# Low halves of some weights made by an accumulating DMA instead of a GpSimd subtraction, in a two-layer hybrid DeltaNet/Hyena/FNet trunk

## The chip, the cores and the metric

One core of one Trainium2 chip. The metric is the device time of one execution in microseconds (us), and what counts is the median over runs.

## The reference, cut to what matters

Two layers with shared weights run over 128 context tokens and 512 latent tokens (640 columns in all, fp32). The first half of each layer multiplies the normalised input `h` by the wide matrix `w_in` and feeds the pieces of the product to three mixers:

```python
proj = h @ p['w_in']                       # columns: qkv | z | b | a | hyena | fnet | 3 gates
y_a, s_fin = delta_mixer(proj[qkv], proj[z], proj[b], proj[a], ...)   # gated DeltaNet, both directions
y_b = hyena_mixer(proj[hyena], ...)
y_c = fourier_mixer(proj[fnet])
merged = gates[0] * (y_a @ w_pa) + gates[1] * (y_b @ w_pb) + gates[2] * (y_c @ w_pc)
x = x + g1 * (merged @ w_o)                # then x = x + g2 * swiglu(norm(x))
```

The DeltaNet is a scan over chunks of 64 tokens, forwards and backwards, and each chunk needs a triangular inverse first.

## The kernel before

**Weights.** A weight matrix comes as blocks of 128 output columns: one transfer of 512 KB on SP's queue into a raw tile `wr` (two buffers). TensorE takes each fp32 operand as a high and a low part in a reduced format (`F32R`), with three matmuls for each product: high by high, high by low, low by high (`mm3`). So each 512-column half of a raw block, called a unit, is split by `wsplit`: ScalarE copies it with rounding into `hi` (tile `wh`), and GpSimd subtracts, `lo = src - hi` (tile `wl`). There are four buffers of each, two blocks' worth. After the last matmuls of a block, `free` emits the splits of the block after the next. A unit is then waiting for TensorE to let go of its buffers, for its raw data, for ScalarE and for GpSimd, in that order.

**The two stretches in question.** After the qkv blocks, `mixer` starts the DeltaNet as four coroutines (`delta`: three of preparation, one scan). While they run, the main program multiplies blocks that don't depend on them: four for the Fourier mixer, four for `z`, twelve for the Hyena input, and eight for the first gate. These 28 blocks of each layer have 56 units, 112 in both layers. The scan's preparation is mostly VectorE work: `delta_inv` inverts the triangular blocks with 110 small elementwise instructions on tiles `A` for each batch, plus 32x32 transposes. GpSimd makes masks and scaled copies for it. VectorE also does the short convolutions of the Hyena blocks (`T<-T,par,T`), whose results SP stores (`hyS`) before it issues the next weight load that stands behind in its queue.

**Order.** The whole program is emitted by a planner at build time: each emitted instruction advances a clock of its engine by a modelled cost (`tick`), and a coroutine's next step is emitted between main-line matmuls when its data should be there by these clocks (`pump`). On the chip each engine works through its own list in that order.

The lines at the centre, from `wsplit`:

```python
nc.scalar.copy(hi[:, :w], src)
nc.gpsimd.tensor_tensor(out=lo[:, :w], in0=src, in1=hi[:, :w].bitcast(F32), op=ALU.subtract)
self.whl[self.nunit] = (hi, lo)
```

The planner's price of a transfer is its bytes at 360 GB/s behind the other transfers, with 2 us to land; that of a GpSimd `tensor_tensor` of 512 columns is 1.24 us.

Of the kernel before, what the change touches and what calls it, by code (L numbers as in the profile page):

```python
# [9 lines left out]
F32 = mybir.dt.float32  # L10
F32R = mybir.dt.float32r
I32 = mybir.dt.int32
AF = mybir.ActivationFunctionType
ALU = mybir.AluOpType
# [5 lines left out]
D = 1024  # L20
# [19 lines left out]
OFF_BA = 2048  # L40
OFF_HY = 2080
OFF_FN = 3616
OFF_G = 4128
# [6 lines left out]
def _stream():  # L50
    s = [("ba", 0)] + [("in", m * P) for m in QKV_ORDER]
    s += [("in", OFF_FN + m * P) for m in range(4)]
    s += [("in", 1536 + m * P) for m in range(4)]
    s += [("in", OFF_HY + m * P) for m in range(12)]
    gate = lambda br, m: ("in", OFF_G + BR[br] * D + m * P)
    s += [gate("a", m) for m in range(8)]
    s += [gate("c", 0), gate("c", 1)]
    s += [("pa", m) for m in range(0, 8, 2)]
    s.append(("pc", 0))
    for m in range(2, 8, 2):  # L60
        s += [gate("c", m), gate("c", m + 1), ("pc", m)]
    s += [gate("b", m) for m in range(8)]
    s += [("pb", m) for m in range(0, 8, 2)]
    s += [("o", m) for m in range(8)]
    for j in range(NFF):
        s += [("g", j), ("u", j)]
    for g in range(len(GROUPS)):
        s += [("d", g, m) for m in range(0, 8, 2)]
    return s


def _plan():

    p = [("w", k) for k in _stream() if k[0] not in ("g", "u", "d")]
    for kind, g in _ffn_order():
        if kind == "gu":
            for j in GROUPS[g]:
                p += [("s", j)] if j >= WHOLE else [("w", ("g", j)), ("w", ("u", j))]
        else:
            p += [("w", ("d", g, m)) for m in range(0, 8, 2)]  # L80
    return p
# [9 lines left out]
def _parked(key):  # L91

    k, m = (key[0], key[-1]) if isinstance(key, tuple) else (None, None)
    return (k == "o" and m >= O_SPLIT or k in ("g", "u") and m == 1 or k == "in" and m // P in QKV_ORDER[1:Q_SPLIT]
            or k == "d" and key[1] == len(GROUPS) - 1 and m >= D_SPLIT)


def _width(key):
    if key[0] == "ba":
        return 256  # L100
    if key[0] == "d":
        return 2 * len(GROUPS[key[1]]) * P
    return 1024
# [195 lines left out]
class _Net:  # L299
# [191 lines left out]
    def wplan(self, depth):  # L491

        keys = {k: n for n, k in enumerate(_stream())}
        self.raws, self.units, self.items = [], [], []
        self.parked = set()
        for l in range(depth):
            for kind, k in _plan():
                r, u = len(self.raws), len(self.units)
                if kind == "w":
                    w = _width(k)  # L500
                    c = 512 if k[0] != "d" else w // 2
                    self.raws.append((l, keys[k], w))
                    self.units += [(r, "raw", i, min(c, w - i)) for i in range(0, w, c)]
                else:
                    self.raws += [(l, keys["g", k], 1024), (l, keys["u", k], 1024)]
                    self.units += [(r, x, 0, 512) for x in SEVEN]
                self.items.append((k, u, len(self.units)))
                if _parked(k):
                    self.parked.update(range(u, len(self.units)))
        self.rlast = {r: n for n, (r, x, *_) in enumerate(self.units) if x[0] != "s"}  # L510
        self.wt = {}
        self.spent, self.sums, self.whl = {}, {}, {}
        self.qs = False
        self.nraw = self.nunit = self.item = self.nseen = self.nout = 0
        self.lot = []
# [26 lines left out]

    def wsplit(self, n):

        nc = self.nc
        while self.nunit <= n:
            r, x, c0, w = self.units[self.nunit]
            self.wload(r if x == "raw" else r + 1)
            if x == "raw":
                src = self.wt[r][:, c0:c0 + w]  # L550
            elif x[0] == "a":
                src = {"a11": self.wt[r][:, :512], "a12": self.wt[r][:, 512:], "a22": self.wt[r + 1][:, 512:]}[x]
            else:
                src = self.wsum(r, x)
            if self.nunit in self.parked:
                hi, lo = self.lot.pop(0)
            else:
                assert self.nout < 4
                self.nout += 1
                hi = self.pw.tile([P, 512], F32R, tag="wh", name=self.nm("wh"), bufs=4)  # L560
                lo = self.pw.tile([P, 512], F32R, tag="wl", name=self.nm("wl"), bufs=4)
            nc.scalar.copy(hi[:, :w], src)
            nc.gpsimd.tensor_tensor(out=lo[:, :w], in0=src, in1=hi[:, :w].bitcast(F32), op=ALU.subtract)
            self.whl[self.nunit] = (hi, lo)
            if x[0] == "a":
                for y in {"a11": ("s2", ), "a22": ("s3", "s4"), "a12": ()}[x]:
                    self.wsum(r, y)
            if self.rlast[r] == self.nunit:
                self.spent[r] = self.spent[r if x == "raw" else r + 1] = self.when(lo)
            if x == "s4":  # L570
                self.sums = {}
            self.nunit += 1
# [1653 lines left out]
```

## Time and profile before

| | |
|---|---|
| median of 3 runs | 2834.18 us (2827.09 to 2837.05) |
| the profiled execution | 2837.89 us, its span 2836.1 us |
| mean granted TensorE clock | 0.949 |
| busy: PE, PEld, DVE, ACT, POOL | 2566.9, 2434.9, 1856.7, 1017.8, 1332.8 us |
| the two stretches (first Fourier block to the output of the DeltaNet) | about 243 to 610 us and 1655 to 2000 us |

PE is TensorE's matmuls, PEld its weight loads, DVE is VectorE, ACT ScalarE, POOL GpSimd, SP the queue that issues most transfers. An arrow `a<-b,c` gives the output and input tiles of an instruction. A wait `X <- Y` is time in which X stood idle and that ended with an instruction of Y. Busy time of a matmul is modelled, and grows when the clock that the chip grants TensorE falls.

### The profile page before, as it was taken

The page shows a single profiled execution, that of the slowest core. Times are in us where ns is not written, and L with a number is a line of the kernel's source. Part 1 is how long each engine was busy: PE and PEld are TensorE (multiplying, and loading weights), DVE is VectorE, ACT ScalarE, POOL GpSimd, SP SyncE. Part 2 cuts the span into 40 slices and gives each one's busy share as a digit, 9 for nine tenths or more (in the row PEclk, how much of TensorE's full clock was granted, in tenths as well). Part 3 has the DMA queues.
Part 4 walks back from the last instruction along what each step waited for, and adds up shares of the span by engine and source line. Part 5 has one row for each costly group of instructions (what it writes and reads, how often), then busy time and mean ns, then how long its engine had stood idle before and what let it go on. Part 6 is the DMA issues. An engine that isn't in the chain of part 4 may idle for free. (4 is left out here: it accounts for less than half of the span.)

```text
span 2836.1 us, 55639 instructions
## 1 busy us (share of the span) xinstructions
PE 2566.9 (91%) x22520; PEld 2434.9 (86%) x22520; DVE 1856.7 (65%) x3417; ACT 1017.8 (36%) x2175; POOL 1332.8 (47%) x1228
## 2 busy tenths in 40 slices
PE   5898779788999999999988979698899989999998
PEld 3687779788998888999977778687889989999997
DVE  5466987544654484767665789784555347877765
ACT  4454224232332342433435532332323323444432
POOL 2234426242335464666742444353423345767662
PEclk8999989899999999999999989798999999999999
DMA  7541221333564246222222312213336442222222
GB/s 288 178 143 56 69 77 56 115 120 122 180 234 148 84 129 216 91 81 89 84 84 97 121 54 79 78 58 98 115 138 243 152 156 65 71 83 83 82 75 82
DMA packets 109552, 324.18 MB, mean 114 GB/s; under 512 B 10202, under 2 KB 24538, under 8 KB 102816
## 3 DMA queue, kind: packets, MB, share of 16 engines
q1 hardware_dynamic: 107856, 312.76, 32.8%
q0 software_dynamic: 1440, 7.87, 0.8%
q8 instruction: 177, 2.90, 0.4%
q14 instruction: 79, 0.65, 0.1%
HBM read 288.60 MB, written 37.24 MB: 115 GB/s over the span
## 5 line engine op out<-in xcount | busy, mean ns | idle before, releaser
L2175 PE MATMUL pg<-A,wh 128*128 128x320 f32 (+1 forms) x6304 | 1473.2, 321 | 52.2 <-DVE T L2175 15.3
L2175 PEld LDWEIGHTS pg<-A,wh 128*128 128x128 f32 (+1 forms) x6304 | 1082.0, 194 | 98.1 <-POOL A L2175 18.6
L2175 POOL TENSOR_TENSOR wl<-wr,wh 128x512 fp32r<-128x512 f32 (+2 forms) x486 | 680.0, 1413 | 769.6 <-ACT wh L2175 730.7
L2175 PE MATMUL pg<-A,wl 128*128 128x320 f32 (+1 forms) x3152 | 997.7, 317 | 0.3 <-POOL wl L2175 0.2
L2175 PEld LDWEIGHTS pg<-A,wl 128*128 128x128 f32 (+1 forms) x3152 | 610.2, 194 | 3.6 <-POOL wl L2175 2.7
L2175 ACT CAST wh<-wr 128x512 fp32r<-128x512 f32 (+2 forms) x486 | 286.3, 612 | 442.9 <-PE pg L2175 341.4
L2175 PE MATMUL ps<-A,wh 128*128 128x320 f32 x1696 | 378.0, 309 | 0.0
L2175 PEld LDWEIGHTS ps<-A,wh 128*128 128x128 f32 x1696 | 283.4, 188 | 1.4 <-issue 1.2
L2175 PE MATMUL ps<-A,wl 128*128 128x320 f32 x848 | 262.9, 310 | 4.6 <-POOL wl L2175 4.4
L2175 PE MATMUL ps<-A,A 32*32 32x32 f32 (+5 forms) x2984 | 215.1, 251 | 52.9 <-DVE A L2175 51.0
L2175 POOL TENSOR_TENSOR wl<-U,wh 128x512 fp32r<-128x512 f32 x160 | 226.6, 1432 | 48.0 <-ACT wh L2175 48.0
L2175 PEld LDWEIGHTS ps<-A,A 32*32 32x32 f32 (+2 forms) x2984 | 186.4, 154 | 66.3 <-DVE A L2175 52.2
L2175 DVE TENSOR_TENSOR A<-A 128x120 f32<-128x120 f32 (+22 forms) x690 | 216.1, 375 | 11.0 <-DMA A<-hyS 8.0
L2175 DVE TENSOR_TENSOR T<-T,T 128x320 f32<-128x320 f32 (+1 forms) x139 | 130.3, 937 | 86.0 <-ACT T L2175 81.8
L2175 POOL TENSOR_TENSOR A<-A,A 128x640 fp32r<-128x640 f32 (+5 forms) x84 | 121.0, 1453 | 112.5 <-ACT A L2175 111.6
L2175 PEld LDWEIGHTS ps<-A,wl 128*128 128x128 f32 x848 | 159.2, 188 | 7.0 <-POOL wl L2175 7.0
L2175 PE MATMUL pg<-A,A 128*128 128x320 f32 x1056 | 160.9, 310 | 0.0
L2175 ACT CAST wh<-U 128x512 fp32r<-128x512 f32 x160 | 99.1, 620 | 162.8 <-PE ps L2175 64.2
L2175 PEld LDWEIGHTS pg<-A,A 128*128 128x128 f32 x1056 | 156.1, 188 | 0.7 <-issue 0.2
L2175 DVE STREAM_TRANSPOSE A<-A 32x1024 f32<-32x1024 f32 x72 | 148.9, 2093 | 1.3
L2175 DVE TENSOR_TENSOR U<-ps,U 128x512 f32<-128x512 f32 x144 | 78.0, 543 | 104.2 <-PE ps L2175 66.3
L2175 DVE SCALAR_TENSOR_TENSOR A<-pg,mod,A 128x320 f32<-128x320 f32 (+2 forms) x152 | 72.8, 492 | 84.9 <-PE pg L2175 84.6
(163 smaller groups left out, 3021.1 us busy)
## 6 DMA issues: line engine op xcount, KB each, us to landing
wr<-in_wbig_dram SPq DMA_DIRECT2D x272, 512.0 KB, 3.6
A<-in_wmod_dram SPq DMA_DIRECT2D x40, 1024.0 KB, 5.3
A<-hT SPq DMA_DIRECT2D x32, 1024.0 KB, 7.1
kSp<-U SPq DMA_DIRECT2D x40, 256.0 KB, 2.1
U<-kSp SPq DMA_DIRECT2D x40, 256.0 KB, 6.0
A<-in_wmod_dram SPq DMA_DIRECT2D x16, 512.0 KB, 10.2
hyS<-T SPq DMA_DIRECT2D x24, 320.5 KB, 3.1
wr<-in_wbig_dram SPq DMA_DIRECT2D x16, 384.0 KB, 3.2
```

The source lines that it names most:

```text
L2175: return f(*a, **k)
```

## The change

For units whose block is in the `z`, Hyena, Fourier or first-gate part of `w_in`, ScalarE first writes `-src`, rounded, into `lo`. Then a transfer issued by GpSimd adds `src` to `lo` in place, from `wr` in on-chip memory to `wl` in on-chip memory, 256 KB each. Only then ScalarE makes `hi`. All other units keep the subtraction.

```diff
+def _added(key):
+
+    return isinstance(key, tuple) and key[0] == "in" and (1536 <= key[1] < OFF_BA or OFF_HY <= key[1] < OFF_G + D)
...
-        self.parked = set()
+        self.parked, self.added = set(), set()
...
+                if _added(k):
+                    self.added.update(range(u, len(self.units)))
...
-            nc.scalar.copy(hi[:, :w], src)
-            nc.gpsimd.tensor_tensor(out=lo[:, :w], in0=src, in1=hi[:, :w].bitcast(F32), op=ALU.subtract)
+            if self.nunit in self.added:
+                nc.scalar.activation(lo[:, :w], src, AF.Copy, scale=-1.0)
+                nc.gpsimd.dma_start(lo[:, :w], src, accum_op=ALU.add)
+                nc.scalar.copy(hi[:, :w], src)
+            else:
+                nc.scalar.copy(hi[:, :w], src)
+                nc.gpsimd.tensor_tensor(out=lo[:, :w], in0=src, in1=hi[:, :w].bitcast(F32), op=ALU.subtract)
```

## Rows read from the trace of the kernel before

**Rows 1.** Busy time by engine, from the page: time, share of the span, instructions.

```profile
PE 2566.9 (91%) x22520; PEld 2434.9 (86%) x22520; DVE 1856.7 (65%) x3417; ACT 1017.8 (36%) x2175; POOL 1332.8 (47%) x1228
```

**Rows 2.** Windows: length, busy PE, PEld, DVE, ACT, POOL; granted clock, DMA share, GB/s.

```profile
243.00:400.00 157.00, 128.07 (x1291) 121.94 (x1293) 135.45 (x302) 47.50 (x108) 73.20 (x89) 0.89 0.23 74
400.00:610.00 210.00, 185.35 (x3192) 172.03 (x3183) 128.55 (x237) 66.83 (x161) 88.85 (x100) 0.91 0.26 83
1655.00:1815.00 160.00, 127.79 (x1349) 121.58 (x1350) 142.99 (x319) 44.10 (x105) 70.09 (x88) 0.86 0.22 71
1815.00:2000.00 185.00, 166.43 (x2934) 155.33 (x2934) 117.19 (x227) 61.41 (x146) 87.55 (x92) 0.92 0.24 74
```

**Rows 3.** Waits of PE, 243 to 400 us: total us, times, longest.

```profile
PE ps L2175 <- DVE A L2175: 13.2, 1, 13.2
PE pg L2175 <- DVE T L2175: 9.3, 6, 3.5
PE ps L2175 <- POOL U L2175: 5.8, 2, 5.6
```

**Rows 4.** Waits of PE, 1655 to 1815 us.

```profile
PE ps L2175 <- DVE A L2175: 14.5, 1, 14.5
PE ps L2175 <- DVE U L2175: 7.6, 2, 7.4
PE pg L2175 <- DVE T L2175: 6.0, 4, 2.8
PE ps L2175 <- POOL U L2175: 5.7, 2, 5.5
```

**Rows 5.** Waits of PE for VectorE, 400 to 610 us, then 1815 to 2000 us.

```profile
PE ps L2175 <- DVE A L2175: 14.1, 7, 4.8
...
PE ps L2175 <- DVE A L2175: 14.6, 6, 5.5
```

**Rows 6.** Groups of VectorE, the inverse's elementwise work: 243 to 400, 1655 to 1815 us.

```profile
L2175 DVE TENSOR_TENSOR A<-A 128x126 f32<-128x126 f32 (+25 forms) x217 | 62.6, 351 | 1.0
...
L2175 DVE TENSOR_TENSOR A<-A 128x126 f32<-128x126 f32 (+25 forms) x217 | 63.6, 356 | 0.9
```

**Rows 7.** The same work by shape, 243 to 400 us, two shapes.

```profile
L2175 DVE TENSOR_TENSOR A<-A 128x128 f32<-128x128 f32 x8 | 1.8, 284 | 0.0
...
L2175 DVE TENSOR_TENSOR A<-A 128x15 f32<-128x15 f32 x2 | 0.3, 171 | 0.0
```

**Rows 8.** Groups of GpSimd, the subtractions, 243 to 400 us.

```profile
L2175 POOL TENSOR_TENSOR wl<-wr,wh 128x512 fp32r<-128x512 f32 x28 | 36.3, 1315 | 51.1 <-ACT wh L2175 42.5 <-PE pg L2175 8.6
```

**Rows 9.** Timeline, 285 us: start, duration, engine, instruction, count.

```profile
284.79 2.48 POOL L2175 TENSOR_TENSOR wl<-wr,wh 128x512 fp32r<-128x512 f32 x2
285.10 4.25 DVE L2175 TENSOR_TENSOR A<-A 128x31 f32<-128x31 f32 x4
```

**Rows 10.** DMA issues: queue, count, KB each, median us from issue to landing.

```profile
A<-in_wmod_dram SPq DMA_DIRECT2D x16, 512.0 KB, 10.2
...
U<-in_cd_dram POOLq DMA_DIRECT2D x2, 256.0 KB, 4.4
U<-in_nptab_dram POOLq DMA_DIRECT2D x2, 256.0 KB, 5.2
```

**Rows 11.** GpSimd's time for issuing such a transfer: ns min/median/max.

```profile
L2175 POOL DMA_DIRECT2D U<-in_cd_dram x2: 607/608/609, 628.2 to 2021.1; - x2
```

**Rows 12.** ScalarE's rounding copies: ns min/median/max.

```profile
L2175 ACT CAST wh<-wr x486: 389/619/757, 36.6 to 2777.3; 128x512 fp32r<-128x512 f32 x150, 128x384 fp32r<-128x384 f32 x10, 128x256 fp32r<-128x256 f32 x2
```

**Rows 13.** Timeline, 355 to 395 us, GpSimd and TensorE's weight loads.

```profile
363.22 2.55 POOL L2175 TENSOR_TENSOR wl<-wr,wh 128x512 fp32r<-128x512 f32 x2 [8.57 <-PE pg L2175]
...
366.65 0.19 PEld L2175 LDWEIGHTS pg<-A,wl 128*128 128x128 f32 x1
...
367.09 0.19 PEld L2175 LDWEIGHTS pg<-A,wl 128*128 128x128 f32 x1
...
384.40 1.60 PEld L2175 LDWEIGHTS ps<-A,A 32*32 32x32 f32 x62 [13.28 <-DVE A L2175]
```

## The prediction

> **What bounds the kernel now.** Start with the page's busy times. TensorE (PE) is busy 91% of the span [rows 1], so over the whole kernel there are some 270 us to win, and only where PE stands still. The windows then show the two stretches in which the 112 affected units are split and used [rows 2]. In the first part of each (243 to 400 us and 1655 to 1815 us) VectorE is busy 135 of 157 and 143 of 160 us, and PE 128 in both, at a granted clock of 0.89 and 0.86. In the second parts PE is busy 88 to 90% of the time and VectorE about 62%. So in the first parts the work that sets the pace is VectorE's, in the second parts mostly PE's. PE's waits say the same [rows 3, 4]: in the first part of layer 0 it waits 13.2 + 9.3 us for VectorE and 5.8 us for GpSimd; in layer 1, 14.5 + 7.6 + 6.0 and 5.7 us. The big single waits of 13 to 15 us end when `delta_inv` has done its second batch. Row [rows 13] shows that place in layer 0: weight loads stop for 13.28 us until 384.40. In the second parts 14.1 and 14.6 us of such waits are left, in pieces of at most 5.5 us [rows 5].
>
> Next, what a subtraction on GpSimd does to VectorE. By shape, an elementwise instruction of the inverse takes 171 ns for 15 elements and 284 ns for 128 [rows 7]: about 156 ns and 1 ns an element. A batch has 110 of them with 10,912 elements (from the loop in `delta_inv`), so a mean of 255 ns when nothing is in the way. The windows show 351 and 356 ns over 217 of them [rows 6]. The excess is (351 - 255) x 217 = 21 us in layer 0 and 22 us in layer 1. What is in the way can be read from the timeline [rows 9]: while GpSimd makes two weight subtractions (2.48 us), four VectorE instructions of 31 elements take 4.25 us, where 4 x 0.187 = 0.75 us were to be expected. So VectorE stands still inside its instructions while GpSimd reads two tiles of on-chip memory.
>
> **The change part by part.**
> *Removed: 112 subtractions.* 28 of them lie in the first part of layer 0, at 1.3 us each, 36.3 of GpSimd's 73 us there [rows 8, 2]; layer 1 does the same work. How much of the 21 and 22 us of excess is theirs? At least their share of GpSimd's busy time, a half: 10.5 and 11 us. At most all of it. They come without regard to what VectorE does, while the scan's own GpSimd work mostly stands before or after the VectorE work of its batch, so I take a value nearer the upper end, 17 us for each layer. The waits for VectorE that it can shorten are 22.5 and 28.1 us in the same windows [rows 3, 4], so it fits into them: 34 us in both layers, with bounds of 21 and 43.
> *Freed: GpSimd's queue.* An issue takes 0.6 us [rows 11] where a subtraction took 1.3, so masks and scaled copies behind it start some 0.7 us sooner for each unit, and PE's two waits for GpSimd (5.8 and 5.7 us, behind two subtractions each) shrink by 1.4 us each. In the second parts the same relief meets a PE that is busy: of 28.7 us of waits for VectorE [rows 5] I count a tenth. Together 3 + 3, say 5 us, with bounds of 0 and 29.
> *Added: 112 rounding copies on ScalarE*, 0.62 us each [rows 12], 69 us. ScalarE is busy 220 of the 712 us [rows 2], so they lie in its idle time. What is queued behind a pair is the eviction of the block's last result and the scan's copies, later by up to 1.2 us. I count nothing; without that cover all 69 us would come on top.
> *Added: 112 transfers.* The trace has none from on-chip memory to on-chip memory and none that adds. The nearest are GpSimd's casting loads of the same 256 KB: 4.4 and 5.2 us from issue to landing [rows 10]. A 512 KB load, which moves the bytes that an add must read, took 10.2 us where it had company [rows 10]. I take 5.2, nearer to the first, since the source is on the chip; 4.4 and 10.2 are the bounds. The low part then is there 0.6 + 5.2 us after ScalarE's write, where the subtraction took 1.3: 4.5 us later. Who waits? PE, if the low part was ready by less than that. In the tightest place of layer 0 that I found, a subtraction pair starts at 363.22, its first unit is done at 364.50, and PE first loads it at 366.65 [rows 13]: 2.15 us of slack, so PE would stand for 2.4 us. But 18 us later PE waits 13 us for VectorE in any case. I allow for two or three like places in each layer. I count 5 us for both layers, between 1 and 8; where the first parts' waits vanish, these stalls are what appears. The raw buffer `wr` is let go 4.5 us later too; its next load stands in SP's queue behind the Hyena stores, which wait for VectorE longer than that, so nothing is added.
> *Not moved on purpose, but moved:* the planner reckons with another price and another engine, so the order of scan steps between the main blocks will differ a little. I have no row for that; it is some us either way.
> *Against:* a rule speaks for a smaller transfer cost than the row. The Trainium skill, DMA: Bandwidth & Descriptors, section Anatomy of one DMA, gives a fit of about 2.0 us and the bytes at 436 GB/s; as an estimate that is 2.6 us for 256 KB. By it no place would run short and the sum would be 5 us lower. The row has 4.4 us for the same size, so the row decides.
>
> **Sum.** -34 - 5 + 5 = -34 us. From the profiled execution, 2837.9 us (span 2836.1 and 1.8 around it), that is 2804. The median of the runs shown is 3.7 us lower, which would give 2800. I forecast 2802 us.
>
> **The rivals.**
> *A, slower: the transfers land too late.* At PE's own pace a block takes 16 weight loads of low parts, 0.44 us apart [rows 13], 7.0 us. A unit's buffers come free up to 1.8 us before the block ends that used them, and it is needed a block later: 8.8 us, of which copy and issue take 1.2. So a landing of L costs nothing up to 7.6 us when blocks follow each other; above that a block loses between half of the rest and all of it (the lead is two blocks), three quarters on the mean. 28 x 7.0 = 197 us of a stretch of 367 are such blocks, so I count half of the 56: 21 x (L - 7.6). With L = 10.2 [rows 10] that is 55 us against 39 gained: 2854. It turns slower than before from L = 9.5. For it: an add reads twice. Against: 4.4 us for a cast of the same size. Chance 0.15.
> The Trainium skill, Collectives: The Full Stack, section The bandwidth ceiling, says that a reducing transfer runs at half the rate of a copy because it needs two source reads. Taken as a doubling of the whole 4.4 us, A would cost 21 x 1.2 = 25 us and the time would be 2824; no trace here shows an add.
> *B, no change: VectorE's time isn't on the path.* The 217 instructions get shorter, but PE fills the time with its own blocks, whose loads pass through SP's queue behind VectorE's convolutions. For it: PE is busy 128 of 157 us; against: the waits of 22 and 28 us. Gain 5, cost 5: 2838. Chance 0.12.
> *C, much faster:* all 43 us of excess go, the second parts' 29 us of waits too, cost 5: 2771. For it the granted clock, 0.85 to 0.93 in these windows, would rise as the waits shrink; against it the second parts' full PE. Chance 0.10.
> *D, the change does only half:* GpSimd's writing of the transfer's descriptors holds VectorE up as its subtraction did, for 0.6 of 1.3 us. Then 18 + 3 - 5 = 16 us: 2822. Chance 0.13.
>
> **How the numbers follow.** My own case has 0.50 and spans 2785 (43 + 5 of gain, 1 of cost, and 6 for the clock) to 2822 (21 of gain, 5 of cost). A change of 0.3%, 8.5 us, is what a measurement here can tell from none. Faster: 0.50 + 0.10 + most of D, 0.71. Same: most of B and some of D, 0.12. Slower: A and the rest of B, 0.17. The range goes down to 2772, which takes in nearly all of C, and up to 2840, which takes in B and leaves out most of A: about 0.18 outside.
>
> **What would show it.** Right: in the first parts the inverse's 217 instructions take about 275 ns instead of 351, the single waits of 13 to 15 us are gone or under 3 us, the second parts hardly change, the transfers land in 4.4 to 6 us, and few new waits of PE name a transfer into `wl`. Wrong: a landing above 7.6 us and PE's weight loads waiting for it (A); waits for VectorE as before, with shorter VectorE work (B); VectorE's instructions still long beside GpSimd's issues (D); or losses outside the two stretches, which only a changed order could explain.

## The result and the profile after

The changed kernel took 2784.23 us (median of 4 runs, 2778.55 to 2790.82) beside 2830.64 us (4 runs) for the kernel before: a ratio of 0.9843, 95% interval [0.9821, 0.9865], so 1.6% or 46 us faster. The forecast was 2802 us and faster, with 2772 to 2840 as its range.

First the page of the changed kernel: the busy times that answer to [rows 1], GpSimd's group of issues, and the transfer's line among the DMA issues (count, KB, median us from issue to landing).

```profile
PE 2552.8 (92%) x22520; PEld 2422.3 (87%) x22520; DVE 1805.7 (65%) x3417; ACT 1076.0 (39%) x2287; POOL 1267.5 (46%) x1228
...
L2188 POOL DMA_DIRECT2D wl<-wr x112 | 98.0, 899 | 272.3 <-ACT wl L2188 258.8
...
wl<-wr POOLq DMA_DIRECT2D x112, 256.0 KB, 4.7
```

VectorE has exactly as many instructions as before, 3417, and needs 51 us less for them: it did the same work with less standing still. TensorE's busy time fell by 14 us at a granted clock of 0.957 (before 0.949). The transfers land in 4.7 us at the median (forecast 5.2); an issue holds GpSimd for 0.90 us (forecast 0.6).

Next the groups of VectorE in the changed kernel, over two spans (240 to 380 us and 1610 to 1760 us) that hold the 217 elementwise instructions of the inverse which [rows 6] counted in each layer, of 331.

```profile
L2188 DVE TENSOR_TENSOR A<-A 128x126 f32<-128x126 f32 (+25 forms) x217 | 46.4, 279 | 1.1
...
L2188 DVE TENSOR_TENSOR A<-A 128x126 f32<-128x126 f32 (+25 forms) x217 | 46.1, 277 | 1.1
```

The mean is 279 and 277 ns where it was 351 and 356: 217 x 72 ns = 15.6 us and 217 x 79 ns = 17.1 us. Behind them, each layer's second part has 114 more instructions of this group. The same view from 1757 to 1930 us:

```profile
L2188 DVE TENSOR_TENSOR A<-A 128x110 f32<-128x110 f32 (+24 forms) x114 | 21.0, 252 | 0.5
```

Here it was 341 ns (from 1815 to 2003 us of the trace before), another 114 x 89 ns = 10.1 us; in layer 0 the same group fell from 322 to 249 ns, 8.3 us. Together that is 51 us, as much as VectorE gained in all.

Then windows of the changed kernel that answer to [rows 2], and TensorE's waits in those four windows (total us, times, longest; they answer to [rows 3 to 5]). The windows don't hold quite the same work as those of before: the first has 1092 matmuls where it had 1291, the second 3390 where it had 3192.

```profile
232.00:365.00 133.00, 118.93 (x1092) 113.08 (x1091) 115.16 (x290) 64.03 (x140) 59.88 (x87) 0.92 0.58 135
365.00:580.00 215.00, 188.59 (x3390) 175.01 (x3389) 133.06 (x268) 86.40 (x203) 76.16 (x108) 0.92 0.47 121
1600.00:1735.00 135.00, 121.47 (x1133) 117.15 (x1132) 121.71 (x321) 66.67 (x141) 56.65 (x85) 0.95 0.56 136
1735.00:1925.00 190.00, 170.20 (x3056) 157.92 (x3056) 125.66 (x270) 77.45 (x184) 68.82 (x98) 0.92 0.48 119
```

```profile
PE ps L2188 <- POOL U L2188: 8.9, 8, 2.8
...
PE ps L2188 <- DVE A L2188: 14.0, 3, 7.2
PE ps L2188 <- DMA A<-in_wmod_dram: 10.2, 5, 4.1
PE pg L2188 <- DMA wl<-wr: 0.7, 1, 0.7
...
PE ps L2188 <- DVE U L2188: 9.6, 3, 6.4
PE pg L2188 <- DMA wl<-wr: 1.0, 1, 1.0
...
PE ps L2188 <- DVE A L2188: 10.3, 3, 5.2
PE pg L2188 <- DMA wl<-wr: 0.9, 1, 0.9
```

So the lengths of the windows (157 and 160 us before, 133 and 135 now) are no measure of the first parts. The inverse's own elementwise instructions are a better mark. In layer 0 its first two batches ran from 282.4 to 402.3 us and now run from 289.3 to 383.3 us, 26 us less; in layer 1 from 1692.0 to 1817.3 us and now from 1665.6 to 1761.2 us, 30 us less. From there to the load of `fnS` behind each stretch it is only 8 and 4 us less (211.8 to 203.6 us, 188.6 to 185.0 us).

The single waits of 13.2 and 14.5 us [rows 3, 4] are shorter, but not gone. In the changed kernel TensorE waits for the inverse inside the second and the fourth window (timeline of its weight loads):

```profile
382.89 1.60 PEld L2188 LDWEIGHTS ps<-A,A 32*32 32x32 f32 x62 [6.14 <-DVE A L2188]
1760.78 1.59 PEld L2188 LDWEIGHTS ps<-A,A 32*32 32x32 f32 x62 [4.40 <-DVE A L2188]
```

Over the whole run, TensorE's waits for VectorE's `A` fell from 64.9 to 33.0 us. TensorE hardly ever waits for a transfer into `wl`: 2.6 us in all four windows. The gain lies inside the two stretches: the first load of `zS`, which marks the end of layer 0's stretch, starts at 579.8 us where it started at 607.1, and a load of `xS` behind layer 1's stretch at 2248.0 where it was 2306.3. So 27 us came from the first and 31 more by the second. These are the two profiled runs, which lie 59 us apart; the medians lie 46 us apart.

### The profile page after: what moved, and what is told of

Read it like the earlier page. It is cut to its first block, busy times and chain, and to the rows that moved or that the text cites. A ratio compares the mean times of both kernels' runs of the same rounds, so it can differ in the third digit from the quotient of the medians.

```text
span 2776.8 us, 55860 instructions
## 1 busy us (share of the span) xinstructions
PE 2552.8 (92%) x22520; PEld 2422.3 (87%) x22520; DVE 1805.7 (65%) x3417; ACT 1076.0 (39%) x2287; POOL 1267.5 (46%) x1228
## 5 line engine op out<-in xcount | busy, mean ns | idle before, releaser
L2188 POOL TENSOR_TENSOR wl<-wr,wh 128x512 fp32r<-128x512 f32 (+2 forms) x374 | 521.7, 1408 | 522.0 <-ACT wh L2188 494.3
L2188 POOL DMA_DIRECT2D wl<-wr x112 | 98.0, 899 | 272.3 <-ACT wl L2188 258.8
L2188 PE MATMUL ps<-A,A 32*32 32x32 f32 (+5 forms) x2984 | 207.3, 241 | 13.6 <-DVE A L2188 10.3
L2188 PEld LDWEIGHTS ps<-A,A 32*32 32x32 f32 (+2 forms) x2984 | 178.8, 144 | 25.4 <-DVE A L2188 10.5
L2188 DVE TENSOR_TENSOR A<-A 128x120 f32<-128x120 f32 (+23 forms) x690 | 163.1, 301 | 11.6 <-DMA A<-hyS 8.2
```

Source lines behind the costliest of these rows:

```text
L2188: return f(*a, **k)
```

## The experiments

Each was compared with runs of the kernel before on the same chip, whose median was 2832.19 us (for experiments 1 to 4), 2829.72 us (5 to 8), 2831.19 us (9 to 11) and 2831.14 us (12). The diffs below are shortened: slices and type casts are left out.

The theory to be tested: the time comes from VectorE, which stands still while GpSimd reads two tiles of on-chip memory for a subtraction. Its rivals: GpSimd's freed queue; the new order of instructions, which the planner made because its prices changed; the place (first or second parts of the stretches). The 95% intervals of the ratios are 6 to 13 us wide to either side, so a difference between two experiments is rough where it is below some 15 us.

**1. The order alone.** The planner reckons as for the change, but the real instructions are the old copy and subtraction.

```diff
+ self.tick("act", "activation", lo, [src]); self.tick("pool", "dma_start", lo, [src])
+ self.tick("act", "copy", hi, [src])
+ nc.scalar._e.copy(hi, src); nc.gpsimd._e.tensor_tensor(lo, src, hi, subtract)
```

> The changed kernel's order of instructions on every engine, but with GpSimd's subtractions as before (and no extra ScalarE copies, no adding transfers). Theory (VectorE is held up by GpSimd's two-input reads): the time of before, 2822 to 2845 us, since the contention is back. Rival 1 (the planner's changed order brings the gain): 2775 to 2795 us. In between by some 10 us if the order has a part.

Measured: 2825.37 us, ratio 0.9984 [0.9964, 1.0005]. The order by itself is worth 5 us, and by the interval it may be nothing.

**2. The instructions alone.** Copy, adding transfer and copy as in the change, in the order of the kernel before (the planner reckons with the old pair).

> The adding transfers of the changed kernel in the order of instructions of the kernel before, on every engine. Theory: 2775 to 2800 us, most of the gain of 46. Rival 1 (order): 2825 to 2840 us.

Measured: 2807.22 us, ratio 0.9906 [0.9881, 0.9932]. That is above the 2775 to 2800 us that the theory gave. So about half of the 46 us is there without the new order, and the order is worth 23 us together with the transfers (18 us by the two ratios), though only 5 us alone.

**3. The reads put back.** The changed kernel, but ScalarE writes half of the negative, and GpSimd adds the low part to itself (two operands of 512 columns) ahead of each transfer.

```diff
- nc.scalar.activation(lo, src, AF.Copy, scale=-1.0)
+ nc.scalar.activation(lo, src, AF.Copy, scale=-0.5)
+ nc.gpsimd._e.tensor_tensor(out=lo, in0=lo, in1=lo, op=ALU.add)
```

> The changed kernel with one more two-input GpSimd instruction of 512 columns for each of the 112 units: ScalarE writes half of -src, GpSimd doubles it in place (lo + lo, 1.3 us), then the transfer is issued. Theory (VectorE is held up by GpSimd's reads of two tiles): the contention is back, and GpSimd's queue and the low parts are 1.3 us later: 2825 to 2850 us. Rival 2 (only the time in GpSimd's queue counts): also slower than 2784, and no slower than the next run, which takes as long in GpSimd's queue without reading.

**4. The same time on GpSimd without reads.** The changed kernel with eight memsets of a scratch tile of 128x32 ahead of each transfer.

> The changed kernel with eight small GpSimd memsets (128x32, some 0.16 us each, 1.3 us in all) ahead of each of the 112 transfers: as long in GpSimd's queue as the run before this one, but they read nothing. Theory: 2780 to 2800 us, near the changed kernel. Rival 2 (time in GpSimd's queue is what counts): 2825 to 2850 us, as the run with the extra read.

Measured: 2861.36 us, ratio 1.0094 [1.0064, 1.0123], for the reads; 2797.45 us, ratio 0.9873 [0.9837, 0.9909], for the writes. The groups of the two kernels, first that with the reads, then that with the writes: the elementwise work over the whole span, and what was put on GpSimd. The last line is the same work in the kernel before.

```profile
L2190 DVE TENSOR_TENSOR A<-A 128x120 f32<-128x120 f32 (+23 forms) x690 | 215.5, 376 | 11.9 <-DMA A<-hyS 8.4
...
L573 POOL TENSOR_TENSOR wl<-wl 128x512 fp32r<-128x512 f32 x112 | 149.5, 1335 | 201.7 <-ACT wl L2190 201.6
```

```profile
L2191 DVE TENSOR_TENSOR A<-A 128x120 f32<-128x120 f32 (+23 forms) x690 | 163.3, 304 | 12.9 <-DMA A<-hyS 8.4
...
L573 POOL MEMSET dmy<- 128x32 f32 x896 | 140.3, 157 | 45.2
```

```profile
L2175 DVE TENSOR_TENSOR A<-A 128x120 f32<-128x120 f32 (+22 forms) x690 | 216.1, 375 | 11.0 <-DMA A<-hyS 8.0
```

149.5 us of reading instructions on GpSimd cost 77 us over the changed kernel and bring VectorE's mean back to 376 ns (before: 375 for the same group); 140.3 us of writing instructions in the same queue cost 13 us and leave it at 304 (changed: 301). So it is the reading that holds VectorE, not GpSimd's time or its queue. This is the run on which the main point rests. The time with the reads is above the theory's 2825 to 2850 us, and not all of the 77 us are VectorE's: the low parts come later too, and TensorE waits 21.2 us for transfers into `wl`, where it waited 2.6.

**5. Neither subtraction nor transfer.** The order of before; three memsets write zeros into each low part, so the low parts are left out of the product. ScalarE makes the high part only.

```diff
- nc.gpsimd._e.tensor_tensor(lo, src, hi, subtract)
+ for c in (512, 512, 384): nc.gpsimd._e.memset(lo[:, :c], 0.0)
```

> Order of the kernel before; for the 112 units GpSimd writes zeros into the low part (three memsets, about 1.3 us, no reading) instead of subtracting; so the low parts of these weights are left out of the product. No extra ScalarE copy, no transfer, low part ready as early as before. Theory: at or below the run with the transfers in this same order (2807): 2795 to 2808 us, and the difference to 2807 is what transfers and extra copies cost. Rival 2 (queue time): 2825 to 2840 us.

Measured: 2766.17 us, ratio 0.9773 [0.9735, 0.9811], clearly under what was expected. The busy times of its page:

```profile
PE 2548.5 (92%) x22520; PEld 2422.6 (88%) x22520; DVE 1792.3 (65%) x3417; ACT 1018.4 (37%) x2175; POOL 1339.0 (48%) x1452
```

Its groups of VectorE over the whole span, the elementwise work and the convolution steps:

```profile
L2190 DVE TENSOR_TENSOR A<-A 128x120 f32<-128x120 f32 (+22 forms) x690 | 174.9, 318 | 10.9 <-DMA A<-hyS 8.0
...
L2190 DVE SCALAR_TENSOR_TENSOR T<-T,par,T 128x641 f32<-128x641 f32 x84 | 88.4, 1053 | 35.1 <-POOL wl L575 15.5 <-POOL wl L2190 7.4 <-ACT T L2190 5.6
```

GpSimd is as busy as before (1339.0 beside 1332.8 us), VectorE's same 3417 instructions take 64 us less, and the time falls by 64 us. Of VectorE's 64 us, 41 are the elementwise work (before 216.1) and 14 the convolutions (before 102.5). So the reads cost about 64 us, and what the change puts in their place gives 41 us back in this order (2807.22 - 2766.17). Two things changed with the reads: the memsets don't wait for ScalarE's high part, and TensorE multiplies by zeros. Neither was tried by itself; TensorE's busy time is only 4 us below that of the changed kernel (2548.5 beside 2552.8 us), so the zeros can't be worth much. In the changed kernel the convolutions take 100.2 us, hardly less than before: their 14 us are lost again.

**6 and 7. One half of the units.** The changed order, with transfers only for the Fourier, `z` and first six Hyena blocks (6), or only for the last six Hyena blocks and the first gate (7); the other units subtract.

> Order of the changed kernel on PE, VectorE and SP; the adding transfer only for the Fourier, z and first six Hyena blocks (56 units, those split while VectorE sets the pace), the subtraction for the other 56. The prediction's theory (the gain comes from the first parts): 2785 to 2798 us. Rival 3 (each unit moved is worth the same, wherever it is): 2800 to 2810 us, midway between 2784 and 2825.

> The reverse: the adding transfer only for the last six Hyena blocks and the first gate (56 units, split where PE sets the pace). The prediction's theory: 2812 to 2828 us, little below the 2825 of the order alone. Rival 3: 2800 to 2810 us.

Measured: 2791.16 us, ratio 0.9855 [0.9809, 0.9901], and 2818.58 us, ratio 0.9951 [0.9933, 0.9969]. Against the order alone (2825) that is 34 us for the first half and 7 us for the second. They add up to the 41 us that both give. So the net gain belongs where VectorE sets the pace. How much of the second half's 7 us is removed reads and how much of them the transfers give back, these runs don't show.

**8. Another price.** The changed kernel, where the planner counts 0.9 us of GpSimd and 4.0 us of landing for each transfer.

> The changed kernel, but its planner prices the adding transfer as the trace shows it (0.9 us on GpSimd, 4.0 us from there to landing, after ScalarE's copy) where it took 0.7 us on the transfers' clock and 2 us. If the changed order helps because it is nearer to what the chip does: 2770 to 2785 us. If the 17 us that the order adds to the transfers are chance: anywhere from 2780 to 2810 us.

Measured: 2786.49 us, ratio 0.9841 [0.9802, 0.988], the same as the change. A price nearer to the trace's doesn't help.

**9. ScalarE's extra copy without a transfer.** As experiment 5, in the order of before, but ScalarE first writes the negative into the low part, GpSimd's memsets then overwrite it, and the high part comes last.

> Before's order, no transfer and no subtraction: as in the run without either (2766 us), the 112 low parts are written with zeros by GpSimd memsets (low parts left out of the product), but ScalarE first writes -w into them, the extra copy that the adding transfer needs, and rounds the high part behind it, as in the changed kernel. That run and the one with the transfers in the same order lie 41 us apart. Theory S (ScalarE's extra copies in front of the high parts give the time back): 2790 to 2807. Theory L (the landing gives it back, ScalarE's copies are hidden, as the prediction has it): 2764 to 2772. Shared: between 2772 and 2790.

**10. A transfer without the extra copy.** In the order of before, ScalarE makes only the high part, and GpSimd issues a plain copying transfer of the raw weights into the low part.

```diff
- nc.scalar._e.activation(lo, src, AF.Copy, scale=-1.0)
- nc.gpsimd._e.dma_start(lo, src, accum_op=ALU.add)
- nc.scalar._e.copy(hi, src)
+ nc.scalar._e.copy(hi, src)
+ nc.gpsimd._e.dma_start(lo, src)
```

> Before's order; ScalarE makes only the high part, and GpSimd issues a plain copying transfer of the raw weights into the low part (the subtraction is left out, so the low part holds w; no extra ScalarE copy). Landing 3 to 5 us. Theory L (landing and issue on GpSimd's queue give back what the removed reads gain): 2795 to 2807, as with the adding transfers. Theory S (the copies on ScalarE do): 2766 to 2780. A theory that the adding is what costs (two reads): landing under 3.5 us and 2766 to 2785.

Measured: 2784.32 us, ratio 0.9836 [0.9814, 0.9859], for the copy; 2786.96 us, ratio 0.985 [0.9827, 0.9872], for the transfer. Over experiment 5 that is 18 and 21 us, 39 together, and both at once had cost 41. Neither theory L nor theory S had it: each part gives back about a half. The theory that the adding is what costs had the short landing right and its upper end, 2785 us, 2 us too low. For the copy, 6 us of the 18 are there when layer 0's stretch ends (579.5 us beside 573.8 for the load of `zS`) and some 7 more only by the start of layer 1's, mostly over work that is the same in both kernels; its clock was 0.953 beside 0.958. So 18 is an upper figure for the copies.

The page of experiment 10, GpSimd's issues and the transfer's landing:

```profile
L574 POOL DMA_DIRECT2D wl<-wr x112 | 61.0, 546 | 247.8 <-PE pg L2189 173.6
...
wl<-wr POOLq DMA_DIRECT2D x112, 256.0 KB, 2.6
```

A plain transfer lands in 2.6 us and takes 0.55 us to issue, and yet it costs 21 us. So a late landing is not the price of the plain transfer.

**11. More units.** The changed kernel with transfers for the query, key and value blocks as well.

> The changed kernel, with adding transfers also for the ten query, key and value blocks of each layer that are not made ahead (40 more units, 152 in all), with an order planned for it. If GpSimd's weight reads cost time wherever VectorE has scan or convolution work, 2772 to 2780 (8 us less for some 0.2 us of excess for each unit). If the gain is bound to the stretches where VectorE sets the pace, 2781 to 2788, as the changed kernel's 2784. If late landings cost there, where PE sets the pace and blocks follow each other, 2790 to 2800.

Measured: 2781.1 us, ratio 0.9832 [0.9809, 0.9856]. That can't be told from the change (0.9843). No run that still makes all low parts beat the changed kernel by more than the measurement is uncertain.

**12. Neither, in the new order.** As experiment 5, but with the order of the change.

> The changed kernel's order (TensorE's and VectorE's instructions in exactly that order), with the cheapest low parts: ScalarE makes the high part only and GpSimd's memsets write zeros (no subtraction, no transfer; low parts left out of the product). The order alone, with the subtractions, gave 5 us. Theory P (the new order is worth some 5 us by itself and, beyond that, hides copies and transfers, so that what they cost in before's order, 18 and 21 us, is mostly gone): 2755 to 2768, against 2784 of the changed kernel. Theory Q (the new order is worth 20 us wherever VectorE isn't held, and copies and transfers cost 40 us in it too): 2738 to 2750. Theory R (in the new order copies and transfers cost nothing): 2778 to 2786.

Measured: 2753.61 us, ratio 0.9723 [0.9696, 0.9751]. It falls between two theories: the order is worth 13 us here, and copies and transfers still cost 31 us in it. That the order is worth 5, 13 or 23 us by what makes the low parts is at the edge of what the intervals can tell. All six corners together, in us:

| low parts made by | order of before | order of the change |
|---|---|---|
| subtraction | 2831 | 2825 |
| adding transfer | 2807 | 2784 |
| memsets (left out) | 2766 | 2754 |

**Where part of the transfers' price lies.** The trace of the changed kernel has a place that the kernel before has not. First the changed kernel, then experiment 12, which has the same order of TensorE's and VectorE's instructions (timeline: start, duration, engine, instruction, count):

```profile
249.70 0.86 POOL L2188 DMA_DIRECT2D wl<-wr  x1 [0.17 <-issue]
...
250.78 8.32 DVE L2188 SCALAR_TENSOR_TENSOR T<-T,par,T 128x641 f32<-128x641 f32 x2 [4.46 <-ACT T L2188]
251.15 2.36 POOL L2188 TENSOR_TENSOR U<-dgh,small 128x512 fp32r<-128x512 f32 x2
...
256.15 1.33 POOL L2188 TENSOR_TENSOR U<-small,dsel 128x512 f32<-128x512 f32 x1
```

```profile
249.02 2.53 DVE L2191 SCALAR_TENSOR_TENSOR T<-T,par,T 128x641 f32<-128x641 f32 x2 [4.29 <-POOL wl L576]
249.83 2.62 POOL L2191 TENSOR_TENSOR U<-dgh,small 128x512 fp32r<-128x512 f32 x2
```

In the changed kernel two convolution steps of VectorE take 8.32 us, as long as GpSimd's run of six back-to-back two-operand instructions (251.15 to 257.5 us); in experiment 12 the same two steps take 2.53 us, of which 1.7 lie beside the same run. At this place the changed kernel loses nothing by it: its TensorE is 1.6 us behind experiment 12's at the same weight load when the hold begins, and 0.4 us behind 20 us later. Experiment 2 shows how such a hold reaches TensorE:

```profile
251.95 0.62 ACT L575 CAST wh<-wr 128x512 fp32r<-128x512 f32 x1
252.35 0.86 POOL L574 DMA_DIRECT2D wl<-wr  x1 [0.17 <-issue]
252.46 0.43 ACT L2190 COPY T<-pg 128x320 f32<-128x320 f32 x1
...
253.43 8.32 DVE L2190 SCALAR_TENSOR_TENSOR T<-T,par,T 128x641 f32<-128x641 f32 x2 [4.97 <-ACT T L2190]
253.80 2.37 POOL L2190 TENSOR_TENSOR U<-dgh,small 128x512 fp32r<-128x512 f32 x2
...
261.85 0.93 ACT L2190 ACTIVATE A<-T 128x256 f32<-128x256 f32 x3 [8.53 <-DVE T L2190]
262.63 0.18 PEld L2190 LDWEIGHTS ps<-small,A 128*128 128x128 f32 x1 [7.45 <-ACT A L2190]
```

Four copies for a block stand on ScalarE in front of the eviction `T<-pg`; so the convolution starts as GpSimd's run begins, is held for its length, and ScalarE and then TensorE wait for it, 7.45 us at the weight load. In the kernel before the same two steps ran from 248.83 us for 2.83 us, and GpSimd's run began at 250.91.

The changed kernel has one that reaches TensorE, at 416.32 us, where GpSimd runs eight such instructions:

```profile
416.32 8.55 DVE L2188 TENSOR_TENSOR A<-A,U 128x256 f32<-128x256 f32 x2
```

TensorE waits 7.25 us for it, until 424.68 us, the longest wait for VectorE in those four windows.

I counted such holds in every trace: VectorE instructions that took over 2.9 us longer than the tenth percentile of their operation and shape in that trace. None of the five kernels without GpSimd transfers into `wl` (before, 1, 5, 9, 12) has one; each of the nine with them has one to six:

| kernel | median us | holds | us in sum |
|---|---|---|---|
| before, 1: subtractions | 2831, 2825 | 0, 0 | 0 |
| 5, 9, 12: no transfer | 2766, 2784, 2754 | 0, 0, 0 | 0 |
| 4: the change, with writes | 2797 | 1 | 6.7 |
| 7: second half of the units | 2819 | 1 | 7.8 |
| 11: more units | 2781 | 2 | 10.0 |
| 6: first half of the units | 2791 | 2 | 13.1 |
| the change | 2784 | 3 | 20.9 |
| 3: the change, with reads | 2861 | 3 | 22.0 |
| 10: plain transfer | 2787 | 4 | 25.6 |
| 8: the change, another order | 2786 | 4 | 28.7 |
| 2: the change in the old order | 2807 | 6 | 40.3 |

The change in the two orders differs by 19.4 us of holds and 23 us of time. But holds and time don't go together throughout: experiment 8 has 8 us more of holds than the change and the same time, experiment 4 has 14 us less and takes 13 us longer.

What a hold costs can be read where two kernels have the same order of TensorE's instructions, by how far one is behind the other at the same weight load, when the hold begins and 20 us later. By that, the three holds of the change cost TensorE 7 of their 20.9 us (against experiment 12); the six of experiment 2 cost 19 of 40.3 us and the four of experiment 10 cost 11 of 25.6 us (against experiment 5). At their ends the three kernels are 25, 42 and 21 us behind. So in experiments 2 and 10 the holds carry about half of the price, in the change about a third. Another part is seen in TensorE's waits for the load `A<-in_wmod_dram`: 35.6 us in the change and 28.9 in experiment 12; 36.9 in experiment 2, 34.5 in experiment 10 and 28.5 in experiment 5. Why that load comes later, and why GpSimd's run lets VectorE in between where no transfer was issued ahead of it, stays open. No run removes the holds alone.

## Why the prediction was right, and where its sizes were off

**What bounds the kernel: right.** The inverse's first two batches took 26 and 30 us less and the second parts 8 and 4, and the half of the units used first gave 34 of 41 us (experiments 6 and 7). One reading was off: the waits of 13 to 15 us don't end with the second batch, since 44 of the 221 elementwise instructions of these batches run after them in either layer. And the sign that was named for them, gone or under 3 us, was not met: 6.1 and 4.4 us are left.

**The subtractions' hold on the inverse: right.** The forecast was 17 us for each layer and 275 ns; measured were 15.6 and 17.1 us, at 279 and 277 ns. Experiments 3 and 4 show the cause: reads on GpSimd hold VectorE, about the same time without reads doesn't.

**What the removed reads are worth in all: mis-sized.** The prediction's terms for what is removed were 34 + 5 = 39 us. Experiments 5 and 12 measured 64 and 72 us. The step that was too small took the excess of the first parts' 217 instructions for all of it. The second parts' 114, 18 us in both layers, were met only by "I count a tenth" of the waits there, and the convolutions, 14 us in experiment 5, by nothing.

**GpSimd's queue: small, as said,** but for another reason: an issue takes 0.90 us, not 0.6, so little is freed. The longest wait for GpSimd in the first part of layer 0 is 2.8 us, where it was 5.6 [rows 3], but there are eight now, 8.9 us in sum where it was 5.8.

**The extra copies on ScalarE at nothing: wrong.** They cost up to 18 us (experiment 9), with 6 in layer 0's stretch, though ScalarE is idle most of the time. The prediction named what is queued behind them, the eviction and the scan's copies, and took a delay of 1.2 us to be free.

**The transfers at 5 us: mis-sized, in the wrong place.** The landing, 4.7 us, was inside the bounds, and TensorE waits 2.6 us for transfers, within the forecast's 1 to 8. But the plain transfers cost 21 us (experiment 10), about half of it through VectorE's long holds; the rest is not traced to one cause. The copies and transfers together gave back 41 us in the old order and 31 in the new, where the forecast had 5.

**The order: "some us either way".** 5 us alone, 13 without reads, 23 with the transfers.

**Sum.** Forecast: 39 gained, 5 lost. In the changed order: 72 gained by removing the reads, 31 given back, 5 from the order: 46. Two terms were too small by 33 and 26 us and mostly cancelled: the direction and the main cause were right, but that the time fell inside the range with these terms was partly luck. Of the 18 us by which 2802 was too high, these terms and the order make 12; the rest is the starting point, some 2836 us where the median of all four runs of before is 2830.64.

**The rivals.** A (late landing): no, 4.7 us at the median and hardly a wait. B (VectorE not on the path): no, TensorE's waits for VectorE's `A` halved and the time fell. C (much faster, 2771): nearer than the main case thought, 13 us away, but not for its reason: of the 43 us of excess in the first parts 33 went, and its cost of 5 us was too small. D (the issue holds VectorE as the subtraction did): not for the inverse, whose mean would have stayed near 310 ns (351 less 9 us over 217); the long holds are another matter.

**The rules weighed.** Experiment 10's plain copy of 256 KB lands in 2.6 us, and 2.6 us is also the estimate by the fit of the Trainium skill, DMA: Bandwidth & Descriptors, section Anatomy of one DMA; the adding transfer of the same size took 4.7 us (4.2 in the old order), 1.6 to 1.8 times that. The half rate that the Trainium skill, Collectives: The Full Stack, section The bandwidth ceiling, states for the reducing step of a collective is near to that, though 1.6 to 1.8 is a ratio of whole times and not of rates.

## What to carry to other kernels

Here 112 two-operand GpSimd instructions of 512 columns were paid for by VectorE, with 64 to 72 us of the kernel's time. Where VectorE sets the pace, price such reads on all of VectorE's instructions in the stretch, not only on the group that shows the excess most clearly. Before pricing the replacement, measure the floor: a kernel with the work left out and the order kept shows how much the replacement gives back, here 41 of 64 us in the order of before, though TensorE waited only 3.9 us for the transfers there. An extra instruction on an engine that is mostly idle isn't free when an eviction stands behind it: here up to 18 us for 112 copies.

## What the runs showed that was not expected

A VectorE instruction can be held for a whole run of GpSimd's reads: 7.40 of the 8.32 us above are its first step, which takes about 0.9 us when free. It was seen in all nine kernels whose GpSimd issued transfers into `wl`, and in none of the other five.

GpSimd's small memsets became slower beside adding transfers. The group in the changed kernel, then in experiment 10 (plain transfers):

```profile
L2188 POOL MEMSET T<- 128x1 f32 x168 | 17.1, 308 | 9.7 <-PE ps L2188 6.5 <-DVE dsel L2188 3.2
```

```profile
L2189 POOL MEMSET T<- 128x1 f32 x168 | 8.7, 106 | 9.6 <-PE ps L2189 6.4 <-DVE dsel L2189 3.2
```

Before it was 98 ns. And an adding transfer took 0.90 us of GpSimd to issue, where a plain one of the same size took 0.55.
